# Attention with value products of two key tiles emitted together, the heads in turn in pieces of 256 columns

## The chip, the cores and the metric

The kernel runs on one core of one Trainium2 chip. The metric is the time of one execution on the device, in microseconds (us). The kernel before was run three times; the times given for it are those three and a fourth execution that was profiled.

## What is computed

The reference runs two transformer blocks over 1024 tokens of width 1024. The change lies in the attention of the first block, which has 16 heads. Cut to what matters:

```python
for blk in range(S // Q_BLOCK):
    ...
    s = jnp.where(k_chunk[None, :] <= q_chunk[:, None], s, -jnp.inf)
    prob = jax.nn.softmax(s, axis=-1).astype(v.dtype)
    outs.append(jnp.einsum('bhqk,bkhd->bqhd', prob, v[:, :q1]))
o = jnp.concatenate(outs, axis=1).reshape(B, S, MLA_WIDTH)
return (o * jax.nn.silu(z)) @ w_out
```

A head has 64 value columns, and a query sees the keys up to its own chunk of 64.

## The kernel before

The first stage makes the projections (`phase1`, `z_tiles`). The attention follows (`attention`, L369 to L608), then the embedding gate (`ple`), the second block with its recurrences (`block2`), a router and the experts (`moe`). The attention goes through eight pairs of heads, `p` from 0 to 7. For each pair two threads of work are emitted side by side: `main2(p)` computes the attention of the pair, and `ahead(p, g)` prepares the next one. It loads weights (`loads`), makes queries and keys (`prep`), takes the row maxima of the scores (`maxima`, matmuls at L469 into the tile `mm`, of which there are two, each read by a VectorE reduction at L471), and every other time the values or the rotated queries. For the last pair the second thread is `ple_start` instead, the first part of the next stage. The function `merge` takes steps from the threads by the costs that they yield, divided by a weight for each thread. That is the order of emission. The order of the instructions on TensorE is made from it by a scheduler, which takes the earliest emitted instruction that its own model holds to be ready. So an instruction that was emitted earlier but was not ready can come to stand between two that were emitted one after the other.

In `main(p)` the scores are transposed: keys lie on the partitions and queries on the columns. A unit is a half of 512 queries (`hf`) and a tile of 128 keys (`j`): four units for the first half, eight for the second, twelve per pair of heads. Each unit has two steps. `score` (L487 to L502) makes, for each of the two heads, a score tile `st` from three matmuls (`mm3`, L152 to L156; three buffers of `st`) and its exponentials on ScalarE (L501) into the tile `p`, 128 x 2 x 512, of which there are three. `value` (L504 to L522) multiplies the exponentials of both heads by the values: one product for each head at L514, with 64 columns of weights, head 0 into partitions 0 to 63 of the tile `o` and head 1 into 64 to 127. The columns left of the causal edge are skipped, so a product has 512, 384, 256 or 128 columns. GpSimd adds the exponentials of all tiles up in `acc` (L517 for the first tile, L519 for the others), and behind the last tile of a half VectorE multiplies `o` by the gate `zs` (L521). `finish` (L524 to L538) turns `acc` into row sums with one product for each head (L527), takes their reciprocals and scales the half. It comes six units later for the first half, and in the next pair's thread for the second (`late`, `last`, `main2`).

The order of the units is one score ahead:

```python
yield from score(*units[0])
late = None
for n, u in enumerate(units):
    if n + 1 < len(units):
        yield from score(*units[n + 1])
    yield from value(*u)
```

Of the kernel before, what the change touches and what calls it, by code (L numbers as in the profile page):

```python
# [15 lines left out]
OP = mybir.AluOpType  # L16
# [80 lines left out]
class Prog:  # L97
# [271 lines left out]
    def attention(self):  # L369
        nc, a, tc = self.nc, self.a, self.tc  # L370
# [18 lines left out]
        V, RQ = {}, {}  # L389
# [90 lines left out]
        def main(p):  # L480
            b, g = p % 2, p // 2
            (qh, ql), (kh, kl) = Q[b], K[b]
            og, zs = {}, {}
            units = [(hf, j) for hf in range(2) for j in range(4 * hf + 4)]
            st = {}

            def score(hf, j):  # L487
                q0 = max(0, j * 128 - hf * 512)
                pt = self.blk("p", 3, shape=(128, 2, 512))
                st[hf, j] = pt  # L490
                if j == 0:
                    zs[hf], og[hf] = self.h5("zs", 2), self.h5("og", 2)
                    nc.sync.dma_start(zs[hf], self.zs_d[p][:, hf * 512:hf * 512 + 512])
                for hh in range(2):
                    ps = self.st()
                    m0 = min(q0, 256)
                    qs = slice(hf * 512 + m0, hf * 512 + 512)
                    ks = slice(j * 128, j * 128 + 128)
                    self.mm3(ps[:, m0:], [x[hh][0:113, ks] for x in (kh, kl)],
                             [x[hh][0:113, qs] for x in (qh, ql)], True, True)  # L500
                    nc.scalar.activation(pt[:, hh, q0:], ps[:, q0:], AF.Exp, scale=SCALE)  # L501
                    yield (512 - m0) * 1.065  # L502

            def value(hf, j):  # L504
                nj = 4 * hf + 4
                q0 = max(0, j * 128 - hf * 512)
                pt = st.pop((hf, j))
                if j == 0:
                    self.o_ps = self.op_()
                    self.acc = self.blk("acc", 2, shape=(128, 2, 512))  # L510
                o, acc = self.o_ps, self.acc
                for hh in range(2):
                    c = (2 * b + hh) * 64
                    nc.tensor.matmul(o[64 * hh:64 * hh + 64, q0:], V[g][j][:, c:c + 64], pt[:, hh, q0:],  # L514
                                     start=j == 0, stop=j == nj - 1)
                if j == 0:
                    nc.gpsimd.tensor_scalar(acc, pt, 1.0, 0.0, op0=OP.mult, op1=OP.add)  # L517
                else:
                    nc.gpsimd.tensor_tensor(acc[:, :, q0:], acc[:, :, q0:], pt[:, :, q0:], op=OP.add)  # L519
                if j == nj - 1:  # L520
                    nc.vector.tensor_tensor(og[hf], o, zs[hf], op=OP.mult)  # L521
                yield (512 - q0) * 1.517  # L522

            def finish(hf, acc):  # L524
                rs = self.st()
                for hh in range(2):
                    nc.tensor.matmul(rs[64 * hh:64 * hh + 64], self.twos, acc[:, hh], start=True, stop=True)  # L527
                yield 910
                rc = zs[hf]
                nc.scalar.activation(rc, rs, AF.Copy)  # L530
                for r in (slice(0, 256), slice(256, 512)):
                    nc.vector.reciprocal(rc[:, r], rc[:, r])  # L532
                nc.gpsimd.tensor_tensor(og[hf], og[hf], rc, op=OP.mult)
                if p < 7:
                    nc.sync.dma_start(self.og_d[p][:, hf * 512:hf * 512 + 512], og[hf])
                else:
                    self.og.setdefault(7, []).append(self.pair((self.A, self.B)[hf](), og[hf]))
                self.dump(f"og{p}_{hf}", og[hf])  # L538

            yield from score(*units[0])  # L540
            late = None
            for n, u in enumerate(units):
                if n + 1 < len(units):
                    yield from score(*units[n + 1])
                yield from value(*u)
                if late and n >= late[0]:
                    yield from finish(*late[1:])
                    late = None
                if u == (0, 3):
                    late = (n + 6, 0, self.acc)  # L550
            self.pending = finish(1, self.acc)

        def last():
# [4 lines left out]
        def main2(p):  # L558
            m = main(p)
            for _ in range(6):  # L560
                yield next(m)
            yield from last()
            yield from m
# [1394 lines left out]
```

## Time and profile before

| | us |
|---|---|
| median of three runs | 2024.95 |
| lowest, highest | 2022.62, 2029.72 |
| the profiled execution, its own time | 2033.76 |
| its span, first to last instruction | 2031.9 |
| TensorE busy | 1918.0 |
| VectorE busy | 1237.9 |
| ScalarE busy | 688.3 |
| GpSimd busy | 599.8 |

The profile is of one execution. Its rows name TensorE's matmuls PE and its weight loads PEld, VectorE DVE, ScalarE ACT and GpSimd POOL. Matmuls are pipelined and their ends are modelled, so a matmul's row reaches into the next one's; what a matmul costs is read from its start to the start of the next. PEclk is the granted share of TensorE's clock.

### The profile page before, as it was taken

Reading aid. Unit: us, or ns where it says so; the run is one execution under the profiler, and the core shown is the slowest. Engines: PE = TensorE matmul, PEld = TensorE weight load, DVE = VectorE, ACT = ScalarE, POOL = GpSimd, SP = SyncE. Lnnn points to the kernel's source line nnn. Section 1 sums busy time; section 2 is a strip of 40 time slices with the busy share of each in tenths; the row PEclk is TensorE's granted clock in tenths of the full one; section 3 lists DMA queues with packets and bytes.
Section 4 is the critical chain, followed back from the end, with each engine's and each line's share of the span. In section 5 each row is a group of like instructions: output and inputs, shape, how many; then the busy total and the mean of one; then the engine's idle time right before and its main releaser. Section 6 shows DMA issues by size and latency. Waiting matters only on the chain. (4 is left out here: it accounts for less than half of the span.)

```text
span 2031.9 us, 27309 instructions
## 1 busy us (share of the span) xinstructions
PE 1918.0 (94%) x10118; PEld 1349.2 (66%) x10118; DVE 1237.9 (61%) x2013; ACT 688.3 (34%) x1261; POOL 599.8 (30%) x425
## 2 busy tenths in 40 slices
PE   8999989999999999999999998999979999999994
PEld 6777556565657788887899998987654444444441
DVE  6765565666654478557754547764566666667653
ACT  5351534444443233344432223342222222222221
POOL 6311344545454435122740224332220100001000
PEclk9999989999999999999999999999979999999997
DMA  4031111101132222433566635565679999999992
GB/s 161 29 99 64 40 42 33 42 33 47 54 104 94 70 79 93 165 102 93 189 216 193 203 124 175 177 193 169 233 257 400 409 410 407 408 408 409 408 408 115
DMA packets 166269, 373.68 MB, mean 184 GB/s; under 512 B 28711, under 2 KB 72487, under 8 KB 166123
## 3 DMA queue, kind: packets, MB, share of 16 engines
q1 hardware_dynamic: 161000, 361.25, 49.7%
q0 software_dynamic: 4096, 8.46, 1.2%
q10 hardware_dynamic: 1024, 2.10, 0.6%
q8 instruction: 82, 1.34, 0.3%
q14 instruction: 67, 0.52, 0.1%
HBM read 314.54 MB, written 59.24 MB: 184 GB/s over the span
## 5 line engine op out<-in xcount | busy, mean ns | idle before, releaser
L148 POOL TENSOR_TENSOR wlo<-wraw,whi 128x512 fp32r<-128x512 f32 (+1 forms) x74 | 105.5, 1427 | 354.0 <-ACT whi L147 314.8
L147 ACT ACTIVATE whi<-wraw 128x512 fp32r<-128x512 f32 (+4 forms) x183 | 103.3, 598 | 301.3 <-PE mm L155 152.8
L519 POOL TENSOR_TENSOR acc<-acc,p 128x1024 f32<-128x1024 f32 (+3 forms) x80 | 144.9, 1811 | 134.7 <-ACT p L501 133.4
L148 DVE TENSOR_TENSOR wlo<-wraw,whi 128x512 fp32r<-128x512 f32 (+4 forms) x109 | 105.8, 974 | 68.1 <-ACT whi L147 67.8
L501 ACT ACTIVATE p<-st 128x512 f32<-128x512 f32 (+1 forms) x192 | 91.2, 490 | 155.6 <-PE st L156 135.4
L471 DVE TENSOR_REDUCE sm<-mm 128x1 f32<-128x128 f32 (+7 forms) x128 | 94.2, 753 | 65.0 <-PE mm L469 64.2
L890 PE MATMUL mm<-whi,A 128*128 128x256 f32 (+1 forms) x640 | 130.1, 292 | 3.4 <-DVE cvx L794 2.4
L890 PE MATMUL mm<-whi,B 128*128 128x256 f32 (+1 forms) x640 | 128.2, 289 | 4.5 <-ACT usw L905 4.1
L514 PE MATMUL o<-p,v 128*64 128x512 f32 (+3 forms) x384 | 117.5, 521 | 3.3 <-ACT p L501 3.3
L1741 POOL TENSOR_TENSOR f<-f,mhalf 128x1 f32<-128x1 f32 (+1 forms) x16 | 8.9, 554 | 359.3 <-DVE f L1740 276.8
L890 PEld LDWEIGHTS mm<-whi,A 128*128 128x128 f32 x640 | 104.1, 192 | 5.4 <-DVE cvx L794 2.6
L890 PEld LDWEIGHTS mm<-whi,B 128*128 128x128 f32 x640 | 102.6, 190 | 6.1 <-ACT usw L905 5.4
L890 PE MATMUL mm<-wlo,A 128*128 128x256 f32 (+1 forms) x320 | 91.7, 287 | 0.0
L154 PE MATMUL mm<-x,whi 128*128 128x512 f32 x208 | 84.1, 405 | 7.4 <-ACT x L132 6.6
L890 PE MATMUL mm<-wlo,B 128*128 128x256 f32 (+1 forms) x320 | 90.6, 283 | 0.0
L155 PE MATMUL mm<-x,whi 128*128 128x512 f32 x208 | 84.4, 406 | 1.8 <-DVE x L133 1.8
L532 DVE RECIPROCAL zs<-zs 128x256 f32<-128x256 f32 x32 | 54.0, 1723 | 50.3 <-ACT zs L530 50.3
L156 PE MATMUL mm<-x,wlo 128*128 128x512 f32 x208 | 83.5, 402 | 0.9 <-DVE wlo L148 0.9
L1699 ACT ACTIVATE gt<-st 128x256 f32<-128x256 f32 x32 | 12.3, 384 | 208.5 <-PE st L1693 208.5
L1700 DVE SCALAR_TENSOR_TENSOR gt<-gt,st 128x256 f32<-128x256 f32 x32 | 13.5, 421 | 113.9 <-ACT gt L1699 113.9
L154 PE MATMUL st<-qk,qk 113*128 113x512 f32 (+1 forms) x192 | 75.9, 395 | 3.1 <-ACT zs L530 2.4
L1693 PE MATMUL st<-E,xT 128*64 128x512 f32 x272 | 77.6, 596 | 0.2 <-SPq L1780 0.2
(524 smaller groups left out, 5273.1 us busy)
## 6 DMA issues: line engine op xcount, KB each, us to landing
B<-in_wexp_dram SPq DMA_DIRECT2D x100, 512.0 KB
E<-in_wexp_dram SPq DMA_DIRECT2D x100, 512.0 KB
A<-in_wexp_dram SPq DMA_DIRECT2D x100, 512.0 KB
F<-in_wexp_dram SPq DMA_DIRECT2D x48, 512.0 KB
wraw<-in_w_dram SPq DMA_DIRECT2D x43, 512.0 KB
wraw<-in_wexp_dram SPq DMA_DIRECT2D x24, 512.0 KB
wraw<-in_wo_dram SPq DMA_DIRECT2D x22, 512.0 KB
u<-usw SPq DMA_DIRECT2D x40, 256.0 KB
```

Source lines behind the costliest of these rows:

```text
L147: nc.scalar.activation(hi[:, r], raw[:, r], AF.Copy)
L148: (nc.vector if i == 0 else eng or nc.gpsimd).tensor_tensor(lo[:, r], raw[:, r], hi[:, r].bitcast(F32), op=OP.subtract)
L154: t.matmul(out, l[0], r[0], start=start, stop=False)
L155: t.matmul(out, l[0], r[1], start=False, stop=False)
L156: t.matmul(out, l[1], r[0], start=False, stop=stop)
L471: nc.vector.tensor_reduce(mc[:, hh * 8 + i:hh * 8 + i + 1], ps[:, :n], axis=AX.X, op=OP.max)
L501: nc.scalar.activation(pt[:, hh, q0:], ps[:, q0:], AF.Exp, scale=SCALE)
L514: nc.tensor.matmul(o[64 * hh:64 * hh + 64, q0:], V[g][j][:, c:c + 64], pt[:, hh, q0:], start=j == 0, stop=j == nj - 1)
L519: nc.gpsimd.tensor_tensor(acc[:, :, q0:], acc[:, :, q0:], pt[:, :, q0:], op=OP.add)
L532: nc.vector.reciprocal(rc[:, r], rc[:, r])
L890: m = t.matmul(ps, x[:, p, ts], w[q][:, k * n:k * n + n], start=u == k == i == 0 and not (shared and tb % 2), stop=u == 1 and k == 3 and i ...
L1693: PE.matmul(gu[64 * e:64 * e + 64], xT[:, k, s:s + 64], w[e][k // 2][:, (k % 2) * 512:(k % 2) * 512 + 512], start=k == 0, stop=k == 7)
```

## The change

The products of two units are emitted together, behind one score and ahead of the other of the next two. Within a unit the columns are cut into pieces of at most 256, and each piece is emitted for head 1 and then for head 0. The row sums of `finish` are cut in the same way. Two scores come ahead of the first products now. Sums, buffers and costs per column stay what they were.

```diff
-            def value(hf, j):
+            def values_(hf, js):
+
                 nj = 4 * hf + 4
-                q0 = max(0, j * 128 - hf * 512)
-                pt = st.pop((hf, j))
-                if j == 0:
+                if js[0] == 0:
                     self.o_ps = self.op_()
                     self.acc = self.blk("acc", 2, shape=(128, 2, 512))
                 o, acc = self.o_ps, self.acc
-                for hh in range(2):
-                    c = (2 * b + hh) * 64
-                    nc.tensor.matmul(o[64 * hh:64 * hh + 64, q0:], V[g][j][:, c:c + 64], pt[:, hh, q0:],
-                                     start=j == 0, stop=j == nj - 1)
-                if j == 0:
-                    nc.gpsimd.tensor_scalar(acc, pt, 1.0, 0.0, op0=OP.mult, op1=OP.add)
-                else:
-                    nc.gpsimd.tensor_tensor(acc[:, :, q0:], acc[:, :, q0:], pt[:, :, q0:], op=OP.add)
-                if j == nj - 1:
-                    nc.vector.tensor_tensor(og[hf], o, zs[hf], op=OP.mult)
-                yield (512 - q0) * 1.517
+                for j in js:
+                    q0 = max(0, j * 128 - hf * 512)
+                    pt = st.pop((hf, j))
+                    for c0, c1 in ((q0, 256), (256, 512)) if q0 < 256 else ((q0, 512),):
+                        for hh in (1, 0):
+                            c = (2 * b + hh) * 64
+                            nc.tensor.matmul(o[64 * hh:64 * hh + 64, c0:c1], V[g][j][:, c:c + 64], pt[:, hh, c0:c1],
+                                             start=j == 0 and c0 == 0, stop=j == nj - 1)
+                    if j == 0:
+                        nc.gpsimd.tensor_scalar(acc, pt, 1.0, 0.0, op0=OP.mult, op1=OP.add)
+                    else:
+                        nc.gpsimd.tensor_tensor(acc[:, :, q0:], acc[:, :, q0:], pt[:, :, q0:], op=OP.add)
+                    if j == nj - 1:
+                        nc.vector.tensor_tensor(og[hf], o, zs[hf], op=OP.mult)
+                yield sum(512 - max(0, j * 128 - hf * 512) for j in js) * 1.517
 
             def finish(hf, acc):
                 rs = self.st()
-                for hh in range(2):
-                    nc.tensor.matmul(rs[64 * hh:64 * hh + 64], self.twos, acc[:, hh], start=True, stop=True)
+                for u in range(2):
+                    for hh in range(2):
+                        nc.tensor.matmul(rs[64 * hh:64 * hh + 64, u * 256:u * 256 + 256], self.twos,
+                                         acc[:, hh, u * 256:u * 256 + 256], start=u == 0, stop=u == 1)
...
-            yield from score(*units[0])
+            for n in range(2):
+                yield from score(*units[n])
             late = None
-            for n, u in enumerate(units):
-                if n + 1 < len(units):
-                    yield from score(*units[n + 1])
-                yield from value(*u)
+            for n in range(0, len(units), 2):
+                nxt = list(units[n + 2:n + 4])
+                if nxt:
+                    yield from score(*nxt[0])
+                yield from values_(units[n][0], [u[1] for u in units[n:n + 2]])
                 if late and n >= late[0]:
                     yield from finish(*late[1:])
                     late = None
-                if u == (0, 3):
+                if units[n + 1] == (0, 3):
                     late = (n + 6, 0, self.acc)
+                if nxt:
+                    yield from score(*nxt[1])
             self.pending = finish(1, self.acc)
```

## Rows read from the trace of the kernel before

**Rows 1.** The page, busy time of each engine over the span.

```profile
PE 1918.0 (94%) x10118; PEld 1349.2 (66%) x10118; DVE 1237.9 (61%) x2013; ACT 688.3 (34%) x1261; POOL 599.8 (30%) x425
```

**Rows 2.** Windows: stretch, length, busy us per engine, PEclk, DMA share, GB/s.

```profile
215.00:625.00 410.00, 394.76 (x1687) 234.50 (x1687) 248.54 (x251) 180.11 (x322) 201.77 (x131) 0.97 0.16 47
625.00:700.00 75.00, 75.00 (x324) 60.53 (x323) 34.00 (x35) 24.89 (x38) 31.44 (x17) 1.00 0.32 102
```

**Rows 3.** Groups by form, 215 to 625 us, L514: busy us, mean ns, idle before.

```profile
L514 PE MATMUL o<-p,v 128*64 128x512 f32 x192 | 81.8, 637 | 3.3 <-ACT p L501 3.3
...
L514 PE MATMUL o<-p,v 128*64 128x384 f32 x64 | 15.5, 508 | 0.0
...
L514 PE MATMUL o<-p,v 128*64 128x256 f32 x64 | 13.4, 412 | 0.0
...
L514 PE MATMUL o<-p,v 128*64 128x128 f32 x64 | 8.5, 293 | 0.0
...
L514 PEld LDWEIGHTS o<-p,v 128*64 128x64 f32 x384 | 26.3, 136 | 37.5 <-issue 27.3 <-ACT p L501 3.7 <-ACT qk L453 1.1
```

**Rows 4.** Timeline of TensorE: start, us, instruction, records; heads side by side.

```profile
248.09 1.08 PE L514 MATMUL o<-p,v 128*64 128x512 f32 x4
249.10 0.56 PE L469 MATMUL mm<-qk,qk 112*128 112x256 f32 x2
...
384.23 1.73 PE L514 MATMUL o<-p,v 128*64 128x512 f32 x8
385.88 0.39 PE L154 MATMUL st<-qk,qk 113*128 113x256 f32 x1
```

**Rows 5.** Timeline of TensorE, stretches of two records.

```profile
218.97 1.07 PE L514 MATMUL o<-p,v 128*64 128x512 f32 x2
...
225.62 1.97 PE L514 MATMUL o<-p,v 128*64 128x512 f32 x2 [3.27 <-ACT p L501]
...
342.50 1.07 PE L514 MATMUL o<-p,v 128*64 128x512 f32 x2
343.50 0.49 PE L469 MATMUL mm<-qk,qk 112*128 112x512 f32 x1
343.92 1.07 PE L514 MATMUL o<-p,v 128*64 128x512 f32 x2
344.93 0.50 PE L154 MATMUL st<-qk,qk 113*128 113x512 f32 x1
...
581.54 1.07 PE L514 MATMUL o<-p,v 128*64 128x512 f32 x2
```

**Rows 6.** Timeline of TensorE's two queues, a stretch of two tiles.

```profile
257.02 0.63 PEld L514 LDWEIGHTS o<-p,v 128*64 128x64 f32 x8 [0.36 <-issue]
257.02 0.87 PE L514 MATMUL o<-p,v 128*64 128x256 f32 x8
...
257.82 0.50 PE L154 MATMUL mm<-c,whi 128*128 128x512 f32 x1
```

**Rows 7.** Timeline of TensorE, full matmuls between two stretches.

```profile
231.38 0.50 PE L154 MATMUL st<-qk,qk 113*128 113x512 f32 x1
231.71 0.39 PE L155 MATMUL st<-qk,qk 113*128 113x512 f32 x1
231.94 0.40 PE L156 MATMUL st<-qk,qk 113*128 113x512 f32 x1
...
232.63 0.40 PE L156 MATMUL st<-qk,qk 113*128 113x512 f32 x1
232.96 0.44 PE L514 MATMUL o<-p,v 128*64 128x128 f32 x4
```

**Rows 8.** Windows, a stretch with maxima beside long tiles (columns as in rows 2).

```profile
342.00:360.00 18.00, 18.00 (x60) 8.20 (x58) 11.27 (x15) 4.75 (x8) 10.24 (x5) 1.00 0.03 12
```

**Rows 9.** Groups by form, 215 to 625 us, GpSimd's sums of tiles of 512.

```profile
L519 POOL TENSOR_TENSOR acc<-acc,p 128x1024 f32<-128x1024 f32 x32 | 78.2, 2444 | 58.3 <-ACT p L501 57.9
```

**Rows 10.** Waits, 215 to 625 us: total, times, longest.

```profile
ACT p L501 <- POOL acc L519: 2.6, 1, 2.6
```

**Rows 11.** Windows, right behind an idle time of TensorE (columns as in rows 2).

```profile
225.61:229.00 3.39, 3.38 (x8) 1.65 (x8) 0.77 (x1) 1.10 (x3) 3.25 (x2) 0.50 0.00 0
```

## The prediction

> **What bounds the kernel now.** I read the shares of the engines first: TensorE is busy for 94% of the span, VectorE for 61% [rows 1]. Then the busy times of the attention stretch, from the first value product to the last row sum, 215 to 625 us: TensorE 394.8 of 410 us, VectorE 248.5, GpSimd 201.8, ScalarE 180.1, at a clock of 0.97; the stage behind it has TensorE busy for 75 of 75 us [rows 2]. So TensorE sets the end of attention, and what it saves there carries over: the later stages start from what this one leaves and nothing in them waits for a fixed moment. Next the groups of TensorE by shape: the value products (L514) hold it for 81.8 + 15.5 + 13.4 + 8.5 us [rows 3]; a product of the code is two records there, 384 for 8 x 12 x 2 products.
>
> The step that matters is the timeline. Where the products of both heads of a tile stand side by side, four records of 512 columns go from 248.09 to 249.10: 1.01 us [rows 4]. Where other work stands between the heads, each head alone takes the same time: 342.50 to 343.50, then 343.92 to 344.93 [rows 5]. So two heads side by side run at once, in the two halves of the array, and the second is free; parted, it costs its full time. The code emits them side by side; the order on the engine is the scheduler's, and it puts a matmul of the maxima (L469) between. I count 129 stretches of value products and row sums in the timeline of TensorE, and 59 of them are of two records, from 218.97 to 581.54 [rows 5]: some 29 tiles of the 96 are parted.
>
> **What a stretch costs beside its columns.** Eight records (512 and 384 columns) take 1.65 us from 384.23 to 385.88 [rows 4]; eight of 256 and 128 take 0.80 us from 257.02 to 257.82 [rows 6]. 512 columns more cost 0.85 us (896 against 384), so 1.66 ns a column of both heads, 0.86 us for 512, and every stretch has 0.15 us on top, whether of four or of eight records. The neighbours pay too: the first full matmul behind a stretch takes 0.33 us to its successor (231.38 to 231.71) against 0.23 for the next one, and the last one ahead 0.33 (232.63 to 232.96) [rows 7]: 0.10 us each. A stretch costs 0.15 + 0.10 + 0.10 = 0.35 us. A tile parted costs 342.50 to 344.93, 2.43 us, less 0.23 for the L469 in it and 1.01 for the whole tile: 1.19 us more than a tile in one piece.
>
> **The change part by part.**
> *Two tiles together.* Between two tiles there is always a score now, so each has a stretch of its own. After it, 48 groups; the row sums are emitted right ahead of or behind one, and I leave 4 stretches for those that don't meet. Of 129 stretches 29 go with the parted tiles, which leaves 100; 100 - 52 = 48 fewer at 0.35 us are **-16.8 us**.
> *Heads in turn.* 29 tiles no longer parted, at 1.19 us, are **-34.5 us**. Together that is -51 us, if nothing else ever stands inside a group.
> *What still stands inside.* A maximum that becomes due while a group runs will cut it, since that is what parts the tiles now. A cut between two pieces of the same columns costs 0.35 us and the 0.43 us for which a piece of 256 columns then runs alone; a cut elsewhere costs 0.35. In a group of two tiles of 512, eight pieces, four of the seven places are of the first kind: 0.35 + 0.57 x 0.43 = 0.60 us. No row shows how often. From below: none, 0. From above: as a tile has one place now and a group seven, twice the 29 of now and a few more, 60: +36 us. I take one per group in the seven head pairs with maxima beside them and the three groups of long tiles of each, and a few more, 24: **+14.4 us**. That is nearer to the lower end, because a maximum waits for its turn of two buffers, and a cycle of two scores now gives several of them room ahead of the group where one score did.
> *More instructions.* The pieces add 256 product records and 64 of row sums. The trace prices them at nothing: the 0.15 us is the same for four records and for eight [rows 4, 6]. The weight loads of those eight take 0.63 us together inside the 0.80 [rows 6], beside matmuls in flight. So I take nothing; what they would cost uncovered is the last rival. The Trainium skill's page "TensorE: Matmul & The Clock Gate" (section "Part 3: Packing small matmuls — row/col tiling") says otherwise: a load overlaps a running matmul only where its row group differs, and these all use all rows; by it the loads would stand on the path, and the sum below would be 9 us of gain, not 31.
> *Moved work.* The sums on GpSimd (L517, L519) and the multiply on VectorE (L521) are issued one tile later; no DMA lies in the moved step. The load of `zs` goes with its score, which is now ahead of the products of one tile more; it is needed only at the end of its half. VectorE's multiply by `zs` must be over before `o` is written again: two scores stand between now, one did. A sum is due as soon as its exponentials are there, which is earlier than its group, so it isn't late; but its buffer of `p` is (rival below).
> *New waits.* TensorE idles 15.2 us of the 410 now. With 36 us less of its own work the others keep theirs, so VectorE goes from 61% of the stretch to 67%. Bounds 0 and 15 (idle doubles); I take **+6**, by the row of the stretch with most maxima, where VectorE has 11.3 of 18 us [rows 8], still with slack.
> Sum: -16.8 - 34.5 + 14.4 + 6 = **-31 us** against the profiled execution of 2033.76 us, so 2003. That one lies 8.8 us above the median of the runs, 2024.95; against the median, **1994 us**. The case's own range: -47 (few cuts, no new idle) to -14 (some 37 cuts and 15 us of new idle), 1978 to 2011.
>
> **Rivals.**
> *The pieces are scattered* (the change doesn't do what it says). For it: the scheduler already parts what the code emits together, and eight pieces give it seven places. Against: groups of eight records of two tiles do stand uncut [rows 4, 6]. With 75 cuts of 0.60 the sum is -51 + 45 + 6 = 0: 2025 us. Chance 0.15.
> *Another engine becomes the bound.* VectorE's maxima need 11.3 us of 18 where TensorE is always busy [rows 8]; if TensorE shrinks to 13 there, every maximum is waited for, and two thirds of the gain turns into a wait: -10, 2015 us. Chance 0.10.
> *Buffers of `p` run out (slower).* There are three. Now two tiles wait for their products and the third is being filled, so the exponentials of the next score can't start before the group has read the oldest tile and GpSimd has added it, 2.44 us per tile of 512 [rows 9]; two in a row are 4.9 us. ScalarE waited for such a sum once, 2.6 us [rows 10]. If each of the 48 groups waits for half a sum, 1.22 us, that is +59: 2053 us. It decides from 31/48 = 0.65 us per group on. Idle time also costs clock: behind 3.27 us without work the two records at 225.62 take 1.97 us instead of 1.07, at a granted clock of 0.50, the lower of the two levels (1.2 GHz) [rows 5, 11]. Against it: 4.9 us of sums stand against 8.5 us per two tiles, the 410 us of attention over 48 groups [rows 2], and 7.8 us after the gain. Chance 0.11.
> *Weight loads are paid.* A load takes 0.136 us [rows 3]; half of the 320 new ones on each half of the array: +22, 2016 us. This is what the rule of the Trainium skill's page above would give. The eight loads inside 0.80 us speak against it: four per half would add 0.54 us to 0.64 of columns. Chance 0.02.
> The forecast has 0.62.
>
> **How the numbers follow.** About 0.3%, 6 us, can be told from no change here. Faster: 0.62, nearly all of the second and fourth rival (0.11) and a quarter of the first (0.04): 0.77. Same: most of what is left of the first, 0.10. Slower: 0.13, the buffers and a little of the first. The range takes the forecast's cases, the second and the fourth rival and the middle of the first: 1978 to 2026 us; about 2 in 10 lie outside.
>
> **What would show it.** In the profile after: value products 640 records; stretches some 75 instead of 129; hardly any two-record stretch of 512 columns; a group of two tiles of 512 from first to next matmul 1.87 us (2 x 0.86 + 0.15); attention some 31 us shorter and the stages behind it as long as before. Wrong would be: L469 inside most groups (scattered), idle of TensorE in attention well above 21 us (another bound), ScalarE waiting for L519 in many groups (buffers), or a group of eight pieces taking longer than its columns and 0.15 us.

## The result, and the profile after

The changed kernel's median is 2000.57 us over four executions (1999.02 to 2007.79). The kernel before has 2027.34 us over four executions on the same chip (the three of the table above are among them; the profiled one is another). The ratio is 0.9875, with a 95% interval of 0.9853 to 0.9897: **26.8 us faster**, where 31 were forecast. In a later comparison, with both kernels again on one chip, it came to 1998.57 us against 2028.08: 0.986 (0.9838 to 0.9883), 29.5 us faster.

In the code after, the products stand at L517 (before L514), the sums of the exponentials at L520 and L522 (L517, L519), the multiply by the gate at L524 (L521), the row sums at L531 (L527) and the copy of the row sums on ScalarE at L535 (L530). The scores (L154 to L156), the exponentials (L501) and the maxima (L469, L471) kept their lines.

The first view is the page's busy time of the engines, which answers to [rows 1]:

```profile
PE 1886.0 (94%) x10438; PEld 1366.6 (68%) x10438; DVE 1245.5 (62%) x2013; ACT 686.7 (34%) x1261; POOL 603.6 (30%) x425
```

TensorE is busy for 32.0 us less, with 320 more matmuls and as many more weight loads. The other engines have the work that they had. The second view is the windows of the attention and of the stage behind it, with the columns of [rows 2]; the attention now ends at 590 us and no longer at 623:

```profile
215.00:591.00 376.00, 359.00 (x2002) 249.59 (x2001) 248.72 (x249) 178.21 (x322) 200.69 (x131) 0.97 0.17 51
590.00:665.00 75.00, 75.00 (x325) 60.29 (x322) 35.03 (x37) 25.90 (x40) 29.50 (x17) 1.00 0.31 99
```

34 us of stretch are gone, and TensorE's idle time is 376.0 - 359.0 = 17.0 us (15.2 before). VectorE's 248.7 us are now 66% of the stretch. So the gain lies in the attention and is TensorE's own work. Third, groups by form of the same stretch, which answer to [rows 3] and [rows 9] (busy us, mean ns, idle before):

```profile
L517 PE MATMUL o<-p,v 128*64 128x256 f32 x512 | 80.3, 406 | 0.0
L522 POOL TENSOR_TENSOR acc<-acc,p 128x1024 f32<-128x1024 f32 x32 | 78.6, 2458 | 31.4 <-ACT p L501 30.4
...
L517 PEld LDWEIGHTS o<-p,v 128*64 128x64 f32 x640 | 40.5, 140 | 35.0 <-issue 21.2 <-ACT p L501 2.2 <-PE mm L469 0.8
L531 PE MATMUL st<-acc,twos 128*64 128x256 f32 x128 | 18.1, 388 | 0.0
L517 PE MATMUL o<-p,v 128*64 128x128 f32 x128 | 14.4, 290 | 0.0
```

The products are 512 + 128 = 640 records, as forecast, and GpSimd's sums cost what they did. The step itself shows in the timeline of TensorE (start, us, instruction, records). First a group of two tiles of 512 columns that nothing parts, then one that is cut three times:

```profile
245.54 1.95 PE L517 MATMUL o<-p,v 128*64 128x256 f32 x16
247.41 0.50 PE L469 MATMUL mm<-qk,qk 112*128 112x256 f32 x2
...
332.57 0.65 PE L517 MATMUL o<-p,v 128*64 128x256 f32 x4
333.15 0.62 PE L469 MATMUL mm<-qk,qk 112*128 112x512 f32 x2
333.69 0.65 PE L517 MATMUL o<-p,v 128*64 128x256 f32 x4
334.28 0.67 PE L469 MATMUL mm<-qk,qk 112*128 112x512 f32 x2
334.88 0.65 PE L517 MATMUL o<-p,v 128*64 128x256 f32 x4
335.46 0.73 PE L469 MATMUL mm<-qk,qk 112*128 112x512 f32 x2
336.13 0.65 PE L517 MATMUL o<-p,v 128*64 128x256 f32 x4
336.71 0.39 PE L469 MATMUL mm<-qk,qk 112*128 112x256 f32 x1
```

The uncut group takes 245.54 to 247.41, 1.87 us, which is 2 x 0.86 + 0.15. In the cut one each piece has four records: both heads of a piece stand together, and four records of 256 columns take 0.58 us (332.57 to 333.15), which is 0.43 + 0.15. The maxima stand between pieces and not between heads. Their six matmuls have 2688 columns, some 1.22 us at the 0.23 us of 512; the group takes 4.14 us from 332.57 to 336.71, so the three cuts cost 4.14 - 1.87 - 1.22 = 1.05 us, 0.35 each. Counted over the attention, the timeline has 96 stretches of products and row sums, of which six have two records (at 226.69, 396.37, 491.56, 517.39, 518.28 and, a row sum, 545.91). Before it had 129, of which 61 had two records: the 59 of the prediction and two of row sums.

Last, what TensorE waited for in the attention (total, times, longest):

```profile
PE st L154 <- ACT p L501: 5.9, 4, 4.5
PE mm L469 <- DVE qk L449: 5.4, 2, 2.8
PE st L154 <- ACT zs L535: 2.0, 1, 2.0
PE mm L469 <- DVE sm L471: 1.8, 3, 0.8
```

The matmuls of the maxima wait less for VectorE's maxima (L471) than before (1.8 us and 5.8), and ScalarE has no wait for GpSimd's sum (L522) any more, where it had one [rows 10].

**Behind the attention** the instructions stand in the same order on every engine. The two first profiles are 32.8 us apart at the end of the attention (623.0 and 590.2) and 26.0 at the end of the span (2031.9 and 2006.0). The difference arises in one stage, from the second block's first transpose to the first expert's matmul: 667.6 us before, 674.1 after. A second profile of the changed kernel has 667.3 us there, and ends at 1995.7; a second one of the kernel before has 663.1. The kernels profiled here, all with the same instructions in that stage, have between 662.6 and 674.1. So those 6.5 us are a difference between executions and not one of the change.

### The profile page after: what moved, and what is told of

Read it like the earlier page. It is cut to its first block, busy times and chain, and to the rows that moved or that the text cites. A ratio compares the mean times of both kernels' runs of the same rounds, so it can differ in the third digit from the quotient of the medians.

```text
span 2006.0 us, 27953 instructions
## 1 busy us (share of the span) xinstructions
PE 1886.0 (94%) x10438; PEld 1366.6 (68%) x10438; DVE 1245.5 (62%) x2013; ACT 686.7 (34%) x1261; POOL 603.6 (30%) x425
## 5 line engine op out<-in xcount | busy, mean ns | idle before, releaser
L522 POOL TENSOR_TENSOR acc<-acc,p 128x1024 f32<-128x1024 f32 (+3 forms) x80 | 143.6, 1795 | 94.0 <-ACT p L501 91.5
L148 DVE TENSOR_TENSOR wlo<-wraw,whi 128x512 fp32r<-128x512 f32 (+4 forms) x109 | 111.6, 1027 | 73.7 <-ACT whi L147 73.6
L501 ACT ACTIVATE p<-st 128x512 f32<-128x512 f32 (+1 forms) x192 | 88.9, 489 | 94.9 <-PE st L156 87.9
L471 DVE TENSOR_REDUCE sm<-mm 128x1 f32<-128x128 f32 (+7 forms) x128 | 94.0, 754 | 38.6 <-PE mm L469 37.0
L154 PE MATMUL mm<-x,whi 128*128 128x512 f32 x208 | 83.8, 403 | 7.0 <-ACT x L132 6.5
L517 PE MATMUL o<-p,v 128*64 128x256 f32 (+1 forms) x640 | 87.1, 383 | 0.0
L156 PE MATMUL mm<-x,wlo 128*128 128x512 f32 x208 | 83.5, 401 | 0.9 <-DVE wlo L148 0.9
L1708 ACT ACTIVATE gt<-st 128x256 f32<-128x256 f32 x32 | 12.3, 384 | 208.8 <-PE st L1702 208.8
L154 PE MATMUL st<-qk,qk 113*128 113x512 f32 (+1 forms) x192 | 71.3, 371 | 8.8 <-ACT p L501 5.9
```

Of the source, the lines that this page charges most:

```text
L148: (nc.vector if i == 0 else eng or nc.gpsimd).tensor_tensor(lo[:, r], raw[:, r], hi[:, r].bitcast(F32), op=OP.subtract)
L154: t.matmul(out, l[0], r[0], start=start, stop=False)
L156: t.matmul(out, l[1], r[0], start=False, stop=stop)
L471: nc.vector.tensor_reduce(mc[:, hh * 8 + i:hh * 8 + i + 1], ps[:, :n], axis=AX.X, op=OP.max)
L517: nc.tensor.matmul(o[64 * hh:64 * hh + 64, c0:c1], V[g][j][:, c:c + 64], pt[:, hh, c0:c1], start=j == 0 and c0 == 0, stop=j == nj - 1)
```

## The experiments

The change does three things: it emits two tiles together (pairing), it cuts the columns into pieces, and it emits head 1 ahead of head 0. The gain could come from any of them. Each run was compared with the kernel before on the same chip; "before" in the table is that median.

| run | us, median | ratio to before (95%) | gain, us | stretches | of them with two records |
|---|---|---|---|---|---|
| pair01 | 2021.55 | 0.9973 (0.9958 to 0.9988) | 6.1 | 104 | 38 |
| pair10 | 2003.14 | 0.9877 (0.9856 to 0.9897) | 24.5 | 87 | 8 |
| order10 | 2004.40 | 0.9894 (0.9873 to 0.9914) | 23.2 | 102 | 8 |
| single | 2006.38 | 0.9897 (0.9878 to 0.9916) | 21.3 | 115 | 5 |
| scoreswap | 2033.74 | 1.0035 (1.0023 to 1.0047) | -8.3 | 122 | 51 |
| swaphalf | 2002.19 | 0.9879 (0.9858 to 0.9899) | 25.9 | 108 | 18 |
| rev10 | 1995.56 | 0.9841 (0.9824 to 0.9858) | 29.9 | 73 | 5 |
| rev10_again | 1994.78 | 0.9839 (0.9821 to 0.9856) | 33.3 | 73 | 5 |
| hp_rev10 | 2015.83 | 0.9940 (0.9926 to 0.9955) | 9.6 | 78 | 6 |
| after_again | 1998.57 | 0.9860 (0.9838 to 0.9883) | 29.5 | 96 | 6 |

### Which of the three parts brings it

**order10** is the kernel before with the two heads of a product emitted the other way round, and nothing else:

```diff
             def value(hf, j):
...
-                for hh in range(2):
+                for hh in (1, 0):
                     c = (2 * b + hh) * 64
```

Expected:

> The kernel before with one edit: within a tile the product of head 1 is emitted ahead of that of head 0; no pairing of tiles, no pieces. Its order on TensorE has 102 column stretches against 129 before and 96 in the changed kernel, and some 4 tiles with parted heads against 29. Theory heads (most of the gain comes from heads that stay side by side, and that comes from head 1 being first, since it waits for the exponentials that are ready last): 27 stretches fewer at 0.35 us and 25 tiles at 0.84 us make attention some 30 us shorter, and the time 22 to 30 us shorter than before. Theory tiles (the gain comes from two tiles in one stretch): under 8 us. Theory pieces (from pieces of 256 columns): no change.

**pair01** is the changed kernel with whole products and head 0 first, so it keeps the pairing and the row sums in pieces:

```diff
-                    for c0, c1 in ((q0, 256), (256, 512)) if q0 < 256 else ((q0, 512),):
-                        for hh in (1, 0):
+                    for c0, c1 in ((q0, 512),):
+                        for hh in (0, 1):
```

Expected:

> The changed kernel with whole products and head 0 first: only the pairing of tiles and the pieced row sums are left. 104 stretches, some 25 tiles with parted heads. Theory heads: 25 x 0.35 + 4 x 0.84 = 12 us shorter in attention, so the time lies 6 to 14 us below the kernel before, half of the change's gain or less. Theory tiles: all of the gain, 22 to 30 us. Theory pieces: no change against before.

**pair10** is the same with head 1 first:

```diff
-                    for c0, c1 in ((q0, 256), (256, 512)) if q0 < 256 else ((q0, 512),):
+                    for c0, c1 in ((q0, 512),):
                         for hh in (1, 0):
```

Expected:

> The changed kernel with whole products instead of pieces of 256, head 1 first. 87 stretches, some 5 tiles with parted heads, 64 x 2 records fewer than with pieces. Theory heads: 42 x 0.35 + 24 x 0.84 = 35 us shorter in attention than before, the same as the changed kernel or up to 3 us better. Theory pieces: 15 us or more slower than the changed kernel, since a cut between the heads now parts 512 columns and not 256.

**single** is the kernel before with the pieces and head 1 first, without the pairing:

```diff
-                for hh in range(2):
-                    c = (2 * b + hh) * 64
-                    nc.tensor.matmul(o[64 * hh:64 * hh + 64, q0:], V[g][j][:, c:c + 64], pt[:, hh, q0:],
-                                     start=j == 0, stop=j == nj - 1)
+                for c0, c1 in ((q0, 256), (256, 512)) if q0 < 256 else ((q0, 512),):
+                    for hh in (1, 0):
+                        c = (2 * b + hh) * 64
+                        nc.tensor.matmul(o[64 * hh:64 * hh + 64, c0:c1], V[g][j][:, c:c + 64], pt[:, hh, c0:c1],
+                                         start=j == 0 and c0 == 0, stop=j == nj - 1)
```

Expected:

> The kernel before with pieces of 256 columns and head 1 first within each tile, tiles not paired. 115 stretches, some 4 parted pieces. Theory heads: 14 x 0.35 + 28 x 0.84 - 4 x 0.43 = 27 us shorter in attention than before, the time 18 to 27 us below before and 5 us above the changed kernel. Theory tiles: no more than 5 us below before. Theory pieces: all of the gain.

The four together are clear. Head 1 first is worth 23.2 us alone, and 18.4 us on top of the pairing (2021.55 to 2003.14, on the same chip). The pairing with head 0 first gives 6.1 us. The pieces give nothing that can be told: single stands beside order10 and the changed kernel beside pair10, with intervals that overlap almost wholly. The pairing on top of head 1 first isn't told from nothing either by the times (pair10 against order10, 1.3 us); in their single profiles pair10's attention ends 7.0 us earlier (588.1 and 595.1), and the later stages of these two executions take it back. Where order10's maxima are due, the timeline of TensorE has the two heads together (four records):

```profile
332.87 1.08 PE L514 MATMUL o<-p,v 128*64 128x512 f32 x4
333.88 0.49 PE L469 MATMUL mm<-qk,qk 112*128 112x512 f32 x1
...
336.83 1.08 PE L514 MATMUL o<-p,v 128*64 128x512 f32 x4
```

pair01, in the same place, has the eight records of a group of two tiles in three stretches, with maxima between them:

```profile
337.20 1.07 PE L517 MATMUL o<-p,v 128*64 128x512 f32 x2
338.20 1.02 PE L469 MATMUL mm<-qk,qk 112*128 112x512 f32 x4
339.15 1.08 PE L517 MATMUL o<-p,v 128*64 128x512 f32 x4
340.16 0.73 PE L469 MATMUL mm<-qk,qk 112*128 112x512 f32 x2
340.83 1.07 PE L517 MATMUL o<-p,v 128*64 128x512 f32 x2
```

The two records at 337.20 take 1.00 us, the four at 339.15 take 1.01 and the two at 340.83 again 1.00. The rows don't name the heads. By the order of emission the first two are head 0 of the first tile, the four are its head 1 beside head 0 of the second tile, and the last two are head 1 of the second. A like stretch of the same trace bears this out: of the four records at 402.53, which take 1.00 us, two have 512 columns and two 384, so they come from two tiles. With head 0 first, pairing alone doesn't stop the parting of a tile's heads; it only lets the two in the middle run side by side.

### Why head 1 first

Head 1 has its exponentials last, so in the kernel before the second product is the one that waits for ScalarE; with head 1 first, both are ready when the first one is. That is one theory ("ready"). The other ("half") is that what counts is the half of the array that the first product uses: head 1 writes the upper half of `o`, partitions 64 to 127. **scoreswap** exchanges the heads in the scores and exponentials of the kernel before. Then head 0's exponentials come last, and head 0's product, in the lower half, still comes first:

```diff
             def score(hf, j):
...
-                for hh in range(2):
+                for hh in (1, 0):
```

Expected:

> The kernel before with one edit in the scores: head 1's score and exponentials come ahead of head 0's, so that the product of head 0, still emitted first, is the one whose exponentials are ready last. 122 stretches, some 25 tiles with parted heads. Theory ready (heads are parted because the second product waits for its exponentials, and head 1 first helps since it has the later wait): as good as head 1 first in the products, 22 to 30 us below before. Theory due (a maximum that becomes due while the first product runs is put in, whatever the second one waits for, unless head 1's product is the first): at most 6 us below before.

**swaphalf** leaves every order as it was before, head 0 first, and exchanges the halves: head 0 writes partitions 64 to 127 and head 1 writes 0 to 63.

```diff
-                    nc.tensor.matmul(o[64 * hh:64 * hh + 64, q0:], V[g][j][:, c:c + 64], pt[:, hh, q0:],
+                    nc.tensor.matmul(o[64 - 64 * hh:128 - 64 * hh, q0:], V[g][j][:, c:c + 64], pt[:, hh, q0:],
...
-                    nc.tensor.matmul(rs[64 * hh:64 * hh + 64], self.twos, acc[:, hh], start=True, stop=True)
+                    nc.tensor.matmul(rs[64 - 64 * hh:128 - 64 * hh], self.twos, acc[:, hh], start=True, stop=True)
```

Expected:

> The kernel before with one edit in the places: the products and row sums of head 0 go to partitions 64 to 127 and those of head 1 to 0 to 63, head 0 still first. The gate isn't moved with them, so the two heads of a pair are gated by each other's gate and the output isn't the reference's; every instruction has the shape and count of before. 108 stretches, some 10 tiles with parted heads. Theory half (the scheduler puts nothing behind a product into the upper half when the next goes to the lower one, whichever head it is): 21 x 0.35 + 19 x 0.84 = 23 us shorter in attention, the time 14 to 23 us below before. Theory head (it is head 1 that must be first): at most 6 us below before.

"Ready" falls: scoreswap gains nothing and is 8.3 us slower. "Half" holds: swaphalf gains 25.9 us, more than was expected of it, with head 0 first and its exponentials first. In the timeline of TensorE scoreswap still parts the heads around the maxima,

```profile
344.61 1.07 PE L514 MATMUL o<-p,v 128*64 128x512 f32 x2
345.62 0.85 PE L469 MATMUL mm<-qk,qk 112*128 112x512 f32 x3
346.40 1.07 PE L514 MATMUL o<-p,v 128*64 128x512 f32 x2
347.40 0.50 PE L154 MATMUL st<-qk,qk 113*128 113x512 f32 x1
```

and swaphalf does not:

```profile
333.79 1.08 PE L514 MATMUL o<-p,v 128*64 128x512 f32 x4
334.80 0.85 PE L469 MATMUL mm<-qk,qk 112*128 112x512 f32 x3
```

This shows that it is the half. Two more traces say the same, if the products are taken in the order of emission (the shapes show that it holds in all but a few places). In pair01 other work stands between the lower half of a tile and its upper half in 37 of 96 places, but between an upper half and the lower half of the group's other tile in 8 of 48. In the changed kernel other work stands between two pieces of one tile, which are ready together, in 14 of 64 places (lower half, then upper), and between the two heads of a piece in 5 of 160 (upper, then lower). Why the scheduler puts hardly anything between an upper and a lower half, and often something between a lower and an upper one, no run shows. Why scoreswap is slower than before (it has 122 stretches, seven fewer, and TensorE idles 20.4 us in the attention, 5 us more) stays open too.

### Can the cuts be avoided as well?

If a group is cut because its second tile isn't ready when its first one is, it should help to emit the later tile's products first, so that the whole group is ready at once. **rev10** does that in pair10, in all groups but the first of a half; GpSimd's sums keep their order:

```diff
-                for j in js:
+                pts = {j: st.pop((hf, j)) for j in js}
+                for j in (js if js[0] == 0 else js[::-1]):
                     q0 = max(0, j * 128 - hf * 512)
-                    pt = st.pop((hf, j))
-                    for c0, c1 in ((q0, 512),):
-                        for hh in (1, 0):
-                            c = (2 * b + hh) * 64
-                            nc.tensor.matmul(o[64 * hh:64 * hh + 64, c0:c1], V[g][j][:, c:c + 64], pt[:, hh, c0:c1],
-                                             start=j == 0 and c0 == 0, stop=j == nj - 1)
+                    for hh in (1, 0):
+                        c = (2 * b + hh) * 64
+                        nc.tensor.matmul(o[64 * hh:64 * hh + 64, q0:], V[g][j][:, c:c + 64], pts[j][:, hh, q0:],
+                                         start=j == 0, stop=j == nj - 2)
+                for j in js:
+                    q0, pt = max(0, j * 128 - hf * 512), pts[j]
```

Expected:

> The changed kernel with whole products, head 1 first, and in each group but a half's first the later tile ahead of the earlier one, so that the first product of a group waits for the exponentials that are ready last. 73 stretches against 96 in the changed kernel and 129 before. Theory heads and stretches (what a stretch costs beside its columns, 0.35 us, comes back for each that goes): 56 x 0.35 + 24 x 0.84 = 40 us shorter in attention than before, 8 us better than the changed kernel, so 30 to 38 us below before. Theory bound (with the heads together another engine sets attention's pace): no better than the changed kernel, within 3 us.

**hp_rev10** is rev10 with the products emitted under the scheduler's high priority, so that they come ahead of any maximum that is due:

```diff
+                with tc.high_priority():
+                    for j in (js if js[0] == 0 else js[::-1]):
...
```

Expected:

> The same as the one with the later tile first, and the products at a high priority for the scheduler, so that no maximum is put ahead of one that is ready. 78 stretches; nearly all groups of two long tiles in one piece. Theory heads and stretches: 6 us better than the changed kernel. Theory bound: the maxima come later, VectorE's reductions bunch up, TensorE waits for them (idle in attention over 20 us), and the time is the changed kernel's or worse.

rev10 has 73 stretches, and its gain of 29.9 us, just under the 30 to 38 that were expected, is the largest of its comparison. Its second run stood beside the changed kernel on one chip:

> The changed kernel, unchanged, for a second profile and for the times on the chip of the version with the later tile first. The kernel before had its attention end at 623.0 and at 615.4 us in two profiles. Theory chance: attention ends within 586 to 596, the stretch from the second block's projections to the experts takes between 663 and 673 and not 674. Theory cause (the change lengthens the later stage): 674 again within 1 us.

> The version with the later tile first, unchanged, beside the changed kernel. Theory stretches: its attention ends 6 to 10 us ahead of the changed kernel's and its time lies 3 to 8 us below it. Theory bound: within 3 us of it.

rev10 came out 3.8 us below the changed kernel there (1994.78 and 1998.57), and its attention ends 3.6 us earlier (583.2 and 586.8), less than expected. The intervals of the two overlap, so "as fast, and probably a little faster" is all that can be said of these two; against the kernel before it is 30 to 33 us faster. Its ratios, 0.9841 (0.9824 to 0.9858) and 0.9839 (0.9821 to 0.9856), do lie clear of order10's 0.9894 (0.9873 to 0.9914), each against the kernel before on its own chip, so pairing with the later tile first (and row sums in pieces) brings some 7 to 10 us beyond head 1 first alone. A group of two whole tiles in the timeline of TensorE of rev10_again takes the same 1.87 us as the changed kernel's pieces:

```profile
377.21 1.94 PE L516 MATMUL o<-p,v 128*64 128x512 f32 x8
379.08 0.50 PE L154 MATMUL st<-qk,qk 113*128 113x512 f32 x1
```

hp_rev10 gives most of it back (it is 20 us slower than rev10), with about as many stretches (78). Part of what it lost is in the waits of TensorE, 215 to 606 us (total, times, longest):

```profile
PE mm L469 <- DVE sm L471: 11.9, 10, 3.8
PE o L517 <- ACT p L501: 7.7, 7, 4.2
PE st L154 <- ACT zs L537: 4.2, 3, 2.9
```

TensorE waits for VectorE's maxima 11.9 us where it waited 1.8 in the changed kernel and 3.3 and 4.3 in the two profiles of rev10. Products that go first hold the maxima back, and VectorE probably gets them late and bunched, with two tiles `mm` to put them in; that reading fits the waits and wasn't tried by itself. TensorE's idle time in the attention is 29.4 us (17.4 and 18.7 in rev10), and 30.7 us of it ran at the lower clock (13.7 in both of rev10). At half speed that is some 8 us more beside the 11 or 12 of idle time, of the 22 to 25 us by which its attention ends later (605.6 us against 580.8 and 583.3).

The last run is the kernel before once more, for a second profile:

> The kernel before, unchanged, for a second profile. From the first matmul of the second block's projections to the first expert matmul the profile of before has 668 us and that of the changed kernel 674, with the same instructions in the same order. Theory chance (this stretch varies from execution to execution): another value within 664 to 676. Theory cause (the change lengthens it): 668 again within 1 us.

It took 2027.16 us, and its attention ends at 615.4 us where the first profile's ends at 623.0, with the same program. The first has 23.9 us of the attention at the lower clock and the second 13.7; at half speed, 10.2 us more of it cost some 5 of the 7.6. So a difference of a few us between two single profiles is no evidence here.

A fourth buffer of `p` wasn't tried. Pieces with head 0 first, and swaphalf with head 1 first, weren't run.

## Why the prediction was right, and where not

**What bounds** held: TensorE's work went down by 32 us and the time by 26.8 and 29.5.

**The prices** held. 0.86 us for 512 columns of both heads and 0.15 us for entering gave 1.87 us for a group of two tiles of 512, and 1.87 was measured, for 16 records and for 8 alike.

**-16.8 us, two tiles together.** This step is half right. The stretches fell from 129 to 96. But order10, with no pairing, has 102: the parted tiles account for most of it. Pairing as such takes the stretches from 102 to 87 (pair10), and its 15 x 0.35 = 5 us aren't told apart in the time (1.3 us).

**-34.5 us, heads in turn.** The size was about right, by luck in part; the cause, as the prediction put it, failed. It held that taking the heads in turn in pieces keeps them together. The kernel before takes them in turn as well, and the pieces change nothing that can be told: what keeps the heads together is that the product of the upper half is emitted first. order10, with that alone, has lost some 26 of the parted tiles (61 short stretches to 8, two for each tile); 26 x 1.19 = 31 us, of which 23 arrived. Some of the rest may be the clock: order10's attention has 27.3 us at the lower level in its one profile, that of the kernel before 23.9 and 13.7 in its two. The prediction read "the heads in turn" in the diff and didn't ask which of them comes first, the one thing in that loop, beside the pieces, that was new.

**+14.4 us, cuts.** The product came out by luck, for both factors were wrong. There are 44 stretches more than the 52 with nothing inside, not 24: by the order of emission 39 of them are cuts inside a group, and nearly all the rest are row sums, which have 10 stretches of their own where 4 were allowed. And a cut costs 0.35 us and not 0.60, because 34 of the 39 stand between pieces whose heads are together: 44 x 0.35 = 15.4 us.

**Nothing for more instructions.** It held. The weight loads are 640 records of 0.140 us, 256 of them new (36 us if these alone were paid), and an uncut group has 16 matmul records with their loads in the 1.87 us that its columns and the 0.15 take. By the rule of the Trainium skill's page "TensorE: Matmul & The Clock Gate" ("Part 3: Packing small matmuls — row/col tiling") on which the last rival stood, that a load overlaps a running matmul only where its row group differs, those loads would have been exposed; here they are not. The same section of the Trainium skill also lets a load be pulled ahead when it goes to a background weight buffer, which the prediction left out and which the 1.87 us don't contradict.

**+6 us, new waits.** It was too much: +2 us between the first profiles (15.2 to 17.0), +3 between the second (12.3 to 15.1).

**The sum.** -51 + 15.4 + 2 = -34, and the attention got 32.8 us shorter between the two first profiles and 28.6 between the two second ones (615.4 and 586.8). That the medians differ by 26.8 and 29.5 us is within what executions of one program vary by in the stages (7.6 us in the attention, 6.5 in the second block).

**The rivals.** Scattered pieces: there are more cuts than forecast, but between the heads hardly any. Another engine as the bound: not in the changed kernel, but the mechanism is there, for hp_rev10 shows it. Buffers of `p`: ScalarE waits for no sum. Paid weight loads: see above.

## What to carry over

Read which instructions stand side by side in the engine's own order, for here a product in one half of the array cost its full 1.00 us alone, and both halves together 1.01; then ask of a diff what changes that order, down to which half is emitted first, and try that one edit alone before a larger one. Keeping products together by priority was no substitute here: it cost 20 us against the same kernel without it. Before a difference of less than 10 us between two profiles is explained, take each program's profile twice.

## What was not expected of the hardware

The same program's attention differed by 7.6 us between two executions, some 5 of them through TensorE's clock. In the first profile of the kernel before, TensorE stood idle for 3.19 us and ran behind it at the lower level, 1.2 GHz (timeline of TensorE, then windows with the columns of [rows 2]):

```profile
294.24 0.69 PE L469 MATMUL mm<-qk,qk 112*128 112x384 f32 x1 [3.19 <-DVE sm L471]
```

```profile
294.00:304.00 10.00, 9.76 (x18) 4.88 (x19) 4.48 (x8) 1.19 (x2) 2.35 (x1) 0.50 0.11 33
```

In its second profile the same matmul came after 2.27 us without work, and the same stretch ran at a mean granted clock of 0.83:

```profile
293.79 0.45 PE L469 MATMUL mm<-qk,qk 112*128 112x384 f32 x1 [2.27 <-DVE sm L471]
```

```profile
294.00:304.00 10.00, 10.00 (x27) 4.08 (x27) 5.90 (x9) 1.79 (x3) 4.43 (x2) 0.83 0.12 33
```

From 294 to 304 us TensorE got through 18 matmul records in the one and 27 in the other. That the idle time is what lowers the clock was not tried by itself; in these two profiles the longer one goes with the lower clock, and it is then worth more than its own 3 us.
